# Three of four transposes of a squared-ReLU MLP's inner values in rounded fp32, from copies that a DMA makes

## The chip, the cores and the metric

The kernel runs on one core of one Trainium2 chip. The metric is the device time of one execution in microseconds; lower is better. Of each kernel several executions are timed, and one more is recorded by the hardware profiler; that one gives the profile and the trace.

The core has a matrix engine (TensorE, PE in the profile; its weight loads are PEld), three engines for vectors (VectorE: DVE, ScalarE: ACT, GpSimd: POOL) and SyncE (SP), which here only issues DMAs. All work from an on-chip memory of 128 partitions; TensorE writes to PSUM banks of 128 x 512 fp32.

## The reference

Two layers over 256 positions of width 2048: in the first the mixer is latent attention, in the second a state-space scan. After each mixer comes a dense MLP with a squared ReLU. Only the two MLPs matter here:

```python
def squared_relu_mlp(h, w_in, w_out):
    u = jax.nn.relu(h @ w_in)
    return (u * u) @ w_out

# in reference(), for each layer i:
    h = rms_norm(x, mlp_norm_g[i])
    x = x + squared_relu_mlp(h, mlp_w_in[i], mlp_w_out[i])   # w_in 2048 x 8192, w_out 8192 x 2048
```

All inputs are fp32.

## The kernel before

**Products in halves.** TensorE multiplies in rounded fp32 (`F32R`). To keep fp32's precision each operand is split into a rounded high half and the rest: ScalarE writes `wh` (L102), VectorE subtracts it and writes `wl` (L103). A product is three matmuls, high x high, high x low, low x high (L594, L595, L596 in the MLPs; L325, L326, L329 elsewhere). The weights come by DMA from SyncE's queue (L85), are split some units ahead, and are the moving operand; the activations are the stationary one, so they have to stand transposed, 128 inner values on the partitions.

**One MLP.** The 8192 inner values are worked on in 8 pairs of blocks of 512, for two halves `t` of the positions. Pair 0 is computed directly (token `c`). Pairs 1 to 7 take seven products of combined quarters in place of eight (tokens `s`, named M1, N7, N5, N6, N4, M2, N3), whose sums VectorE forms (`sub` and `plus`, L598 and L599). The quarters of the weights are combined by VectorE (L183) and, once for each of four steps, by a DMA of GpSimd that adds to a tile (L199). Between the tokens of pair p run those of the out-projection of the pair before (`o`, four column blocks, of which the last falls into the pair after).

**A turn.** When the sums of a block are there, ScalarE takes the ReLU (L602) and the square (L546, in `hidden`) in a 128 x 512 scratch tile `r`. A *turn* then brings the tile into the stationary form: `transposed` (L306 to L311) makes four transposes of 128 x 128 on TensorE (L310) into one PSUM bank of the pool `sm`, and `split_out` has ScalarE write the high half (L299) and VectorE the low half (L300). There are four turns in a pair, for e, w, m1 and c in the code's names: after N6, N4, M2 and N3. `transpose` is given the data and the fp32 identity `self.ident`.

**The order.** TensorE runs in the order in which the program is written; that of the other engines is made by the compiler's scheduler, from the order of the program. `plan()` writes out the order of the tokens. `mlp_body` goes through them with a clock of its own, `at[0]`, which `move` advances by TensorE's time of the products (1.36 us for an `s` token, 2.72 for the others). `turn` (L578) puts the transposes on a list with a due time: the clock plus 10, 8, 7, 7 or 5 us (`TR`), and at least 4 us (`TR_GAP`) after the turn before. `move` issues whatever is due after a token.

**Buffers.** The pool `sm` has two banks; the turns and N7's accumulation share them. A bank is free when both halves have been written from it. The pool `mp` belongs to one MLP; the scratch tiles `s2` are seven.

Of the kernel before, what the change touches and what calls it, by code (L numbers as in the profile page):

```python
# [20 lines left out]
F32 = mybir.dt.float32  # L21
F32R = mybir.dt.float32r
# [6 lines left out]
P = 128  # L29
# [185 lines left out]
class Trunk:  # L215
# [90 lines left out]

    def transposed(self, src, h, lo, wide=True):
        b = self.bank(wide)
        for j in range(4):
            self.nc.tensor.transpose(b[:, j * P:(j + 1) * P], src[:, j * P:(j + 1) * P], self.ident)  # L310
        self.split_out(h, lo, b.rearrange("p (k n) -> p k n", k=4))  # L311


# [225 lines left out]
    def mlp_body(self, mp, layer, gain):  # L539
        nc = self.nc  # L540
        xa, rs = self.xT, self.rs
        us = {}

        def hidden(r, pp, j, t):

            nc.scalar.activation(r, r, AF.Square)  # L546
            if (pp, j) not in us:
                us[pp, j] = (self.ktile(self.k4), self.ktile(self.k4))
            h, lo = us[pp, j]
            return lambda wide: self.transposes(r, h, lo, t, wide)  # L550

        def relu(src, t):
# [12 lines left out]
        out, bank, v, count = {}, {}, {}, {}  # L565
        due = []
        at = [0.0, 0.0]
# [10 lines left out]
        def turn(r, p, j, t, us):  # L578

            fn = hidden(r, p, j, t)  # L580
            at[1] = max(at[0] + us, at[1] + TR_GAP)
            due.append((at[1], lambda: fn(False)))

        def pair_of_banks(pool):
# [20 lines left out]
        def after(name, p):  # L605
            if name == "M1":
                v["m1"] = self.scratch()
                nc.scalar.activation(v["m1"], bank["M1"], AF.Copy)
            elif name in ("N5", "N6"):
                v[name] = p  # L610
                if v.get("N5") != p or v.get("N6") != p:
                    return
                w, c, e = (self.scratch() for _ in range(3))
                sub(w, bank["N6"], v["m1"])
                plus(c, bank["N5"], w)
                plus(w, bank["N7"], w)
                plus(e, bank["N7"], c)
                v["w"], v["c"] = w, c
                turn(relu_in_place(e, 1), p, 1, 1, TR[0])
            elif name == "N4":  # L620
                sub(v["w"], bank["N4"], v["w"])
                turn(relu_in_place(v["w"], 1), p, 0, 1, TR[1])
            elif name == "M2":
                plus(v["m1"], bank["M2"], v["m1"])
                turn(relu_in_place(v["m1"], 0), p, 0, 0, TR[2])
            elif name == "N3":
                plus(v["c"], bank["N3"], v["c"])
                turn(relu_in_place(v["c"], 0), p, 1, 0, TR[3])
# [5 lines left out]
        for tok in tokens:  # L634
            key = (tok[0], layer) + tok[1:]
            if tok[0] == "s":
                _, p, name, d = tok
# [12 lines left out]
            elif tok[0] == "c":  # L650
                _, p, j, o = tok
# [11 lines left out]
            else:  # L663
                _, p, nb, o = tok
# [701 lines left out]
LATE5 = ()  # L1366
TR = (10, 8, 7, 7, 5)
TR_GAP = 4
PAUSE = 2.7


def merged(p, blocks):
# [21 lines left out]
    while main or late or second or units:  # L1394
        op = next((q for q in (late, main, second) if q and ready(*q[0])), None)
        filler = t >= rest and len(units) > (4 if p == 7 and op else 0)
        if filler and (op is None or work > t * ve / pe - 2):
# [3 lines left out]
            if not units or units[0][0] != b:  # L1401
                rest, work = t + (PAUSE if b[0] == "o" else 10), work + 1.37
        else:
# [160 lines left out]
```

## Time and profile before

| | us |
|---|---|
| median of 3 runs | 2293.53 (2292.96 to 2295.82) |
| the profiled execution | 2294.05 |
| its span, first to last instruction | 2292.3 |
| DVE (VectorE) busy | 1907.0 |
| ACT (ScalarE) busy | 1392.6 |
| POOL (GpSimd) busy | 212.7 |

The page has busy times, the span in 40 slices, the DMA queues, the chain of work that ended last, the costliest groups of instructions and the DMA issues. A group's row gives the line, the engine, what is written and read, the shape and the count; then busy time and the mean duration of one in ns; then the idle time of the engine before them and what ended it. Matmuls are pipelined: a record's duration is longer than the distance to the next start. In a timeline the columns are start, duration, engine, line, operation and count.

### The profile page before, as it was taken

The numbers are of one execution on the slowest core, as the hardware profiler recorded it, in microseconds if no ns is written. First come the engines' busy times: TensorE is split into PE (matmuls) and PEld (weight loads), VectorE is DVE, ScalarE is ACT, GpSimd is POOL, SyncE is SP. The second block draws the span as 40 slices with busy tenths as digits, with TensorE's granted clock in tenths as the row PEclk, the third lists the DMA queues.
The fourth block names the chain that finished last, engine by engine and source line by source line (L and its number), as shares of the span: only waits on it lengthen the run. The fifth ranks groups of instructions, "written<-read, shape, count | busy, mean of one in ns | idle before, by whom it ended". The sixth has DMA issues, their size and how long they took to land.

```text
span 2292.3 us, 30455 instructions
## 1 busy us (share of the span) xinstructions
PE 2283.9 (100%) x10929; PEld 1898.4 (83%) x10929; DVE 1907.0 (83%) x2318; ACT 1392.6 (61%) x1947; POOL 212.7 (9%) x229
## 2 busy tenths in 40 slices
PE   9999999999999999999999999999999999999999
PEld 7898888888888888888888888888888888888887
DVE  7785698999899898687898688676989889989895
ACT  7775476566566666564666545544666666666663
POOL 1430000000000000000133112120000000000000
PEclk9999999999999999999999999999999999999999
DMA  8445687877887878667877777666687788888874
GB/s 315 151 126 155 198 230 249 261 242 252 262 242 247 262 215 275 201 209 241 283 262 264 253 265 256 228 197 200 208 258 233 244 267 244 249 267 239 249 226 163
DMA packets 161912, 538.07 MB, mean 235 GB/s; under 512 B 17680, under 2 KB 26832, under 8 KB 160736
## 3 DMA queue, kind: packets, MB, share of 16 engines
q1 hardware_dynamic: 151264, 502.44, 66.2%
q0 software_dynamic: 8096, 29.41, 7.9%
q10 hardware_dynamic: 2400, 4.27, 0.5%
q8 instruction: 86, 1.41, 0.3%
q14 instruction: 66, 0.54, 0.1%
HBM read 529.65 MB, written 6.41 MB: 234 GB/s over the span
## 4 chain that ended last, share of the span: by engine, by line
PE 97%; DMA 1%; DVE 1%; issue 0%; ACT 0%; SPq 0%; DVEq 0%
PE acc L325 13%; PE acc L326 13%; PE acc L329 13%; PE yp L595 9%; PE yp L596 9%; PE yp L594 9%; PE st L595 7%; PE st L596 7%; PE st L594 7%; PE sm L310 2%; DMA wraw<-mi 1%; DVE wl L103 1%; PE y L1280 1%; PE acc L594 1%; PE acc L596 1%; PE acc L595 1%
## 5 line engine op out<-in xcount | busy, mean ns | idle before, releaser
L102 ACT ACTIVATE wh<-wraw 128x1024 fp32r<-128x1024 f32 (+1 forms) x818 | 858.2, 1053 | 607.3 <-PE acc L326 284.3
L103 DVE TENSOR_TENSOR wl<-wraw,wh 128x1024 fp32r<-128x1024 f32 (+1 forms) x818 | 986.4, 1221 | 230.2 <-ACT wh L102 220.8
L595 PE MATMUL yp<-wl,k 128*128 128x512 f32 x896 | 348.9, 389 | 2.0 <-DVE wl L103 2.0
L594 PE MATMUL yp<-wh,k 128*128 128x512 f32 x896 | 349.8, 390 | 0.0
L596 PE MATMUL yp<-wh,k 128*128 128x512 f32 x896 | 348.8, 389 | 0.0
L325 PE MATMUL acc<-wh,xt 128*128 128x512 f32 x704 | 279.1, 397 | 0.9 <-ACT wh L102 0.9
L326 PE MATMUL acc<-wh,xt 128*128 128x512 f32 x704 | 274.5, 390 | 0.3 <-DVE xt L463 0.3
L102 ACT ACTIVATE wh<-wrx 128x1024 fp32r<-128x1024 f32 x168 | 177.9, 1059 | 136.0 <-PE yp L596 107.1
L103 DVE TENSOR_TENSOR wl<-wrx,wh 128x1024 fp32r<-128x1024 f32 x168 | 204.4, 1222 | 35.6 <-ACT wh L102 35.3
L595 PEld LDWEIGHTS yp<-wl,k 128*128 128x128 f32 x896 | 168.2, 188 | 37.4 <-DVE wl L103 2.8
L596 PEld LDWEIGHTS yp<-wh,k 128*128 128x128 f32 x896 | 168.2, 188 | 35.0
L594 PEld LDWEIGHTS yp<-wh,k 128*128 128x128 f32 x896 | 168.2, 188 | 34.7
L325 PE MATMUL acc<-wh,k 128*128 128x512 f32 x496 | 196.5, 396 | 0.0
L326 PE MATMUL acc<-wh,k 128*128 128x512 f32 x496 | 193.2, 390 | 0.0
L329 PE MATMUL acc<-wl,xt 128*128 128x512 f32 x704 | 188.3, 389 | 0.0
L594 PE MATMUL st<-wh,xt 128*128 128x512 f32 x448 | 176.8, 395 | 0.0
L595 PE MATMUL st<-wl,xt 128*128 128x512 f32 x448 | 174.8, 390 | 0.0
L596 PE MATMUL st<-wh,xt 128*128 128x512 f32 x448 | 174.8, 390 | 0.0
L325 PEld LDWEIGHTS acc<-wh,xt 128*128 128x128 f32 x704 | 132.3, 188 | 29.9 <-ACT wh L102 2.2
L326 PEld LDWEIGHTS acc<-wh,xt 128*128 128x128 f32 x704 | 132.3, 188 | 28.5 <-issue 1.2
L329 PEld LDWEIGHTS acc<-wl,xt 128*128 128x128 f32 x704 | 132.2, 188 | 27.7
L199 POOL DMA_DIRECT2D wrx<-mi x56 | 49.1, 876 | 1142.1 <-DVE wl L103 1036.1
(307 smaller groups left out, 3447.9 us busy)
## 6 DMA issues: line engine op xcount, KB each, us to landing
wraw<-mi SPq DMA_DIRECT2D x256, 512.0 KB, 5.3
wraw<-mo SPq DMA_DIRECT2D x256, 512.0 KB, 5.5
wraw<-si SPq DMA_DIRECT2D x160, 512.0 KB, 4.9
wraw<-so SPq DMA_DIRECT2D x64, 512.0 KB, 4.8
wrx<-mi SPq DMA_DIRECT2D x56, 512.0 KB, 5.3
wrx<-mi POOLq DMA_DIRECT2D x56, 512.0 KB, 8.2
wraw<-wo SPq DMA_DIRECT2D x32, 512.0 KB, 3.8
taps<-xD SPq DMA_DIRECT2D x16, 768.0 KB, 8.7
```

The source lines that it names most:

```text
L102: self.last = nc.scalar.activation(h[:, v], raw[:, v], AF.Copy)
L103: self.last_lo = nc.vector.tensor_tensor(lo[:, v], raw[:, v], h[:, v].bitcast(F32), ALU.subtract)
L199: nc.gpsimd.dma_start(st["b11"].tile, quarter(d, 1, 0), accum_op=ALU.add)
L310: self.nc.tensor.transpose(b[:, j * P:(j + 1) * P], src[:, j * P:(j + 1) * P], self.ident)
L325: nc.tensor.matmul(accs[t][:, :n], ah, wh[:, q, :], start=first and kt + q == 0, stop=False)
L326: nc.tensor.matmul(accs[t][:, :n], al, wh[:, q, :], start=False, stop=False)
L329: nc.tensor.matmul(accs[t][:, :n], lhs(kt + q, t)[0], wl[:, q, :], start=False, stop=en and q == nk - 1)
L594: nc.tensor.matmul(b, ah, wh, start=first and q == 0, stop=False)
L595: nc.tensor.matmul(b, ah, wl, start=False, stop=False)
L596: nc.tensor.matmul(b, al, wh, start=False, stop=last and q == 1)
L1280: nc.tensor.matmul(y[t][c, o], part(t)[:, c], xg[g][t][:, o], start=True, stop=True)
```

## The change

In pairs 1 to 6 of each MLP, once the square is there, GpSimd's DMA copies the first 384 of the 512 columns, word for word, into a tile of type `F32R` (four buffers). The turn's first three transposes read that tile, use an identity in `F32R` and write the bank as `F32R`; the fourth reads `r` in plain fp32 as before. The due time of these turns is 8 us later. The identity is copied once per MLP by GpSimd. Pairs 0 and 7 and all other transposes stay as they were.

```diff
     def transposed(self, src, h, lo, wide=True):
         b = self.bank(wide)
+        src, words = src if isinstance(src, tuple) else (src, None)
         for j in range(4):
-            self.nc.tensor.transpose(b[:, j * P:(j + 1) * P], src[:, j * P:(j + 1) * P], self.ident)
+            v = slice(j * P, (j + 1) * P)
+            if words is not None and j < 3:
+                self.nc.tensor.transpose(b.bitcast(F32R)[:, v], words[:, v], self.ident_r)
+            else:
+                self.nc.tensor.transpose(b[:, v], src[:, v], self.ident)
         self.split_out(h, lo, b.rearrange("p (k n) -> p k n", k=4))
...
         us = {}
+        self.ident_r = mp.tile([P, P], F32R, name="identr")
+        nc.gpsimd.tensor_copy(self.ident_r, self.ident)
...
             h, lo = us[pp, j]
+            if pp in WORDS:
+                q = mp.tile([P, 384], F32R, tag="tr", name=self.name("tr"), bufs=4)
+                nc.gpsimd.dma_start(q.bitcast(F32), r[:, :384])
+                r = (r, q)
             return lambda wide: self.transposes(r, h, lo, t, wide)
...
             fn = hidden(r, p, j, t)
-            at[1] = max(at[0] + us, at[1] + TR_GAP)
+            at[1] = max(at[0] + us + (COPY if p in WORDS else 0), at[1] + TR_GAP)
             due.append((at[1], lambda: fn(False)))
...
 TR_GAP = 4
+WORDS = range(1, 7)
+COPY = 8
 PAUSE = 2.7
```

## The prediction

> **What bounds the kernel now.** I read the page first (busy shares, granted clock, the chain that ended last), with the group of the transposes from the view by line and shape; then what the engines waited for; then the timeline of TensorE around one turn.
>
> ```profile
> PE 2283.9 (100%) x10929; PEld 1898.4 (83%) x10929; DVE 1907.0 (83%) x2318; ACT 1392.6 (61%) x1947; POOL 212.7 (9%) x229
> PEclk9999999999999999999999999999999999999999
> PE 97%; DMA 1%; DVE 1%; issue 0%; ACT 0%; SPq 0%; DVEq 0%
> ```
> ```profile
> L310 PE MATMUL sm<-cst,s 128*128 128x128 f32 x396 | 57.1, 272 | 0.0
> ```
>
> TensorE is busy for the whole span, at full clock, and the chain is 97% TensorE. So time goes only with TensorE's own instructions, and with waits that it does not have now. The transposes at L310 are a small group: 57.1 us for 396, and not all are touched.
>
> ```profile
> PE yp L595 <- DVE wl L103: 2.0, 2, 1.1
> DVE wraw L183 <- DMA wraw<-mi: 24.2, 24, 3.6
> ```
>
> In the MLPs TensorE waited only twice, 2.0 us in all, for a low half of a weight. VectorE waited 24 times for late weights, 24.2 us in all, and nearly all of it was absorbed before it reached TensorE.
>
> A matmul's record holds its pipeline latency, so what it costs is the distance between starts. This is one turn (four transposes between ordinary products):
>
> ```profile
> 644.26 0.39 PE L595 MATMUL yp<-wl,k 128*128 128x512 f32 x1
> 644.48 0.39 PE L596 MATMUL yp<-wh,k 128*128 128x512 f32 x1
> 644.71 0.60 PE L310 MATMUL sm<-cst,s 128*128 128x128 f32 x4
> 645.07 0.48 PE L594 MATMUL yp<-wh,k 128*128 128x512 f32 x1
> 645.38 0.39 PE L595 MATMUL yp<-wl,k 128*128 128x512 f32 x1
> 645.62 0.40 PE L596 MATMUL yp<-wh,k 128*128 128x512 f32 x1
> ```
>
> Ordinary starts lie 0.227 us apart. From 644.71 to 645.38 there are 0.67 us, of which one product takes 0.227: a turn costs about 0.45 us. The four records last 0.60 in sum and 272 ns each by the L310 row, so the starts lie (600 - 272) / 3 = 109 ns apart. A turn is four times 109 ns and some 15 ns at the change.
>
> **The change, part by part.** Pairs 1 to 6 of two layers, four turns in each: 48 turns, in each of which three of the four transposes change type. So 144 transposes count.
>
> *The shorter transposes.* No row shows a transpose of rounded fp32, so I go by how the moving columns are priced in the two types. L344 and L596 move rounded fp32; L932 and L1232 move plain fp32.
>
> ```profile
> L596 PE MATMUL yp<-wh,k 128*128 128x512 f32 x896 | 348.8, 389 | 0.0
> ...
> L1232 PE MATMUL sm<-s,cb 128*128 128x512 f32 x16 | 8.2, 590 | 0.0
> ...
> L344 PE MATMUL sm<-xt,wh 128*128 128x256 f32 x32 | 4.2, 283 | 0.0
> ...
> L932 PE MATMUL sm<-xt,xt 128*128 128x128 f32 x16 | 3.1, 273 | 0.0
> ```
>
> Plain: (590 - 273) / 384 = 0.83 ns a column. Rounded: (389 - 283) / 256 = 0.41 ns, half. The transpose of today (272) sits on the plain line (273 for the same 128 columns), and its distance, 109 ns, is 128 columns at 0.83 and next to nothing more. What does the rounded line give for the distance?
>
> ```profile
> 29.23 2.08 PE L344 MATMUL sm<-xt,wh 128*128 128x256 f32 x16
> ```
>
> (2080 - 283) / 15 = 120 ns for 256 columns and 227 ns for 512: 107 ns for 256 more, and 13 ns that do not depend on the columns. For 128 columns that is 53 + 13 = 66 ns. The other bound comes from the weight loads.
>
> ```profile
> L310 PEld LDWEIGHTS sm<-cst,s 128*128 128x128 f32 x396 | 48.3, 141 | 9.9
> ...
> L932 PEld LDWEIGHTS sm<-xt,xt 128*128 128x128 f32 x32 | 5.4, 191 | 0.4
> L344 PEld LDWEIGHTS sm<-xt,wh 128*128 128x128 f32 x32 | 4.1, 191 | 0.2
> ```
>
> A transpose's load is recorded with 141 ns, a rounded product's with 191. If a rounded transpose loads like a product, the load may set the pace, and all that the rows say is that it is no slower than L344's 120 ns. So the distance lies between 53 ns (columns alone) and 120 ns. I take 66: plain products have the 191 ns load too, so the shorter load goes with the transposing and not with the type. Saving: 3 x (109 - 66) = 0.13 us a turn, **6.2 us** over 48 turns. By the ends: 8.1 us saved, or 1.6 us lost.
>
> The Trainium skill speaks against this: "TensorE: Matmul & The Clock Gate", part 4 on the PE-mode transpose, puts a transpose at about 275 ns in a kernel and 173 of these down to access latency that dominates. The 272 ns agree, but by the 109 ns between starts the latency is overlapped; by the page alone the saving would be near nothing.
>
> *The word copy.* In each turn GpSimd issues a DMA of 128 x 384 words (192 KB) from the squared values, after ScalarE's square, and three transposes wait for its landing.
>
> ```profile
> wrx<-mi POOLq DMA_DIRECT2D x56, 512.0 KB, 8.2
> ...
> xD<-s POOLq DMA_DIRECT2D x1, 48.0 KB, 2.6
> ```
>
> GpSimd's transfers land in 2.6 us (48 KB) and 8.2 us (512 KB, adding to what is there). In proportion 192 KB give 2.6 + 5.6 x 144 / 464 = 4.3 us, an estimate; the ends are 2.6 and 8.2. The Trainium skill, "DMA: Bandwidth & Descriptors", anatomy of one DMA on the SWDGE path, would give 2.0 us and 0.45 us for the bytes; the 8.2 us, for which it would give 3.2, say that here it is too little.
>
> How much time is there? Pair 4, first layer: the squares on ScalarE and the turns on TensorE (the third, at 644.71, stands above).
>
> ```profile
> 624.54 0.63 ACT L546 ACTIVATE s<-s 128x512 f32<-128x512 f32 x1
> ...
> 634.55 0.63 ACT L546 ACTIVATE s<-s 128x512 f32<-128x512 f32 x1
> ...
> 640.16 0.62 ACT L546 ACTIVATE s<-s 128x512 f32<-128x512 f32 x1
> ...
> 646.97 0.62 ACT L546 ACTIVATE s<-s 128x512 f32<-128x512 f32 x1
> ```
> ```profile
> 627.45 0.60 PE L310 MATMUL sm<-cst,s 128*128 128x128 f32 x4
> 638.80 0.60 PE L310 MATMUL sm<-cst,s 128*128 128x128 f32 x4
> 649.27 0.60 PE L310 MATMUL sm<-cst,s 128*128 128x128 f32 x4
> ```
>
> Square's end to turn: 2.3, 3.6, 3.9 and 1.7 us. Following the planner's clock (1.36 us a token of a combined product, 2.72 of another; a turn goes out at the first token past its due time), COPY = 8 moves the first three turns of a pair by six tokens' worth, 8.16 us, and the fourth, which also has to keep TR_GAP, by 9.52. So the copy has 10.4, 11.8, 12.1 and 11.2 us. It needs 4.3, at most 8.2: **no wait**. The cover ends at a landing 10.4 us after the square.
>
> *GpSimd's queue.* Behind a waiting copy stand the adding DMAs of L199, on which the N4 products depend.
>
> ```profile
> 614.26 0.88 POOL L199 DMA_DIRECT2D wrx<-mi  x1 [18.24 <-DVE wl L103]
> 654.46 0.87 POOL L199 DMA_DIRECT2D wrx<-mi  x1 [39.32 <-DVE wl L103]
> ```
>
> Between 614.26 and 654.46 GpSimd did nothing, and all four squares of the pair end in that time (625.2 to 647.6). An issue takes 0.87 us. Cost: none.
>
> *The later turns.* Each turn takes one of two small banks and gives it back when VectorE has written the low half (L300).
>
> ```profile
> 647.15 0.69 DVE L300 TENSOR_TENSOR k<-sm,k 128x512 fp32r<-128x512 f32 x1
> ...
> 652.29 0.69 DVE L300 TENSOR_TENSOR k<-sm,k 128x512 fp32r<-128x512 f32 x1
> ```
>
> From a turn's start to that: 3.1 us (644.71 to 647.84) and 3.7 us (649.27 to 652.98). With the shift the third and fourth turns of a pair fall behind the start of the next pair's N7, which holds the other bank for long, so both use one bank, 5.44 us apart by the planner (4.08 in pair 6) and a turn's 0.33 us more: enough by 2 us, in pair 6 by 0.7. The out products that read the values now come 8.16 us after the third turn (6.8 in pair 6) and not 16.3: also enough. I cost both at nothing; were VectorE 3 us later, each of 12 pairs would lose up to 1 us.
>
> *The waits themselves.* Transposes now wait for a DMA too.
>
> ```profile
> L310 PEldq EVENT_SEMAPHORE  x76: 51/51/1211, 45.4 to 2240.5; - x76
> ```
>
> Such a wait takes 51 ns in the sequencer; the turn above lost nothing by it on the way in (644.48 to 644.71 is an ordinary step). Between 66 ns transposes it might show: 0 to 48 x 51 ns = 2.4 us. I take 0, as in the turns of today.
>
> *The transfers.* 48 x 192 KB run beside the weight loads.
>
> ```profile
> 641.00:651.00 10.00, 10.00 (x50) 8.29 (x49) 10.00 (x11) 6.47 (x9) 0.00 (x0) 1.00 0.65 206
> 651.00:661.00 10.00, 10.00 (x46) 8.28 (x45) 9.91 (x11) 6.39 (x7) 0.87 (x1) 1.00 0.74 197
> ```
>
> The DMA share is 0.65 and 0.74 where the last two copies of a pair run, so there is room; but the next pair's first weights are those for which VectorE waits already, and 192 KB at some 300 GB/s hold them up by 0.65 us. In 12 pairs that is 0 to 7.8 us; only the 2 waits that reach TensorE today have no cover, so I take two such places at 0.5 us: **+1.0 us**.
>
> *The rest:* the rounded identity is one small copy per MLP on an idle GpSimd, the first turn that needs it comes, by the planner, some 90 us later; nothing.
>
> **Sum.** The profiled execution took 2294.05 us (span 2292.3 and 1.75 around it). 2294.05 - 6.2 + 1.0 = 2288.85. It lies 0.5 us above the median of 2293.53, so on the median's scale about **2288.4 us**, 0.22% less. The bound that a measurement can tell is 0.2%, 4.6 us: the line lies at 2288.9, and my forecast hardly passes it.
>
> **The rivals.**
> - *The transposes get no shorter.* The load of 191 ns, or a transposing rate that does not depend on the type, keeps the distance at 109 to 120 ns. For it: the two load rows, and that no row shows such a transpose (also the skill's rule above). Against: half the price of a column in each rounded row. Time: 2293.5 + (0 to 1.6) + 1.0, so 2294 to 2296.
> - *The gain goes into new waits.* Turns 1 us late in one bank, or 0.65 us of late weights in more pairs, or 51 ns in each turn. For it: VectorE is full in 641 to 651 (10.00 of 10.00). Against: margins of 2 us. Time: 2288.4 + 2 to 5, so 2290.5 to 2293.5.
> - *The copies are late; slower.* TensorE stops in order at the transposes. The loss of a pair is what the landing exceeds 10.4, 11.8, 12.1 and 11.2 us by, summed. At 10.8 us it eats the gain (0.4 x 12 = 5 us); at 11.5 us it is 1.4 x 12 = 17 us: 2305; at 12.5 us 4.5 x 12 = 54 us. For it: GpSimd's transfers are the slowest of all in the list of DMAs beside their size. Against: 8.2 us for over twice the bytes.
>
> **How the numbers follow.** Forecast 0.54, of which 0.42 on the far side of 2288.9 and 0.12 on the near side, since the 53 ns end and an absent wait pull down (to 2285) and the 51 ns up. No shorter: 0.19, of which 0.03 over 2298.1 (with late weights in several pairs). New waits: 0.14, all within. Late copies: 0.13, slower. So faster 0.42, within 0.2% 0.42 (0.12 + 0.16 + 0.14), slower 0.16. The range runs from 2285.0 (8.1 us saved, nothing lost) to 2297.5, leaving out the late copies and little else. The forecast's own range is 2285.0 to 2290.5.
>
> **What would show it.** Right: the three transposes start 66 ns apart and a turn costs 0.32 us, not 0.45; copies land in 3 to 6 us, TensorE has no wait for them; the waits of L595 for L103 stay at 1 to 4 us. Wrong: a distance of 109 or more; waits of TensorE at the transposes named by the copy's DMA, or by L300; a longer list of waits for late weights.

## The result

| | before | changed |
|---|---|---|
| median of 10 runs, us | 2294.13 (2292.39 to 2296.86) | 2288.68 (2286.92 to 2289.81) |
| span of the profiled execution, us | 2292.3 | 2287.5 |

The ratio is 0.9974, 95% interval 0.9965 to 0.9984: 3.7 to 8.0 us less. (The ten runs of before, on the chips of this comparison, have a median 0.6 us above the three that the prediction started from.) The forecast was 2288.4.

The page of the changed kernel, busy shares and chain, then the transposes in the view by line and shape (L313 the rounded ones, L315 the plain ones):

```profile
PE 2280.0 (100%) x10929; PEld 1893.7 (83%) x10929; DVE 1906.0 (83%) x2318; ACT 1391.2 (61%) x1947; POOL 243.0 (11%) x279
...
PE 95%; DVE 2%; DMA 2%; ACT 1%; issue 1%; POOL 0%; SPq 0%; ACTq 0%; DVEq 0%
```
```profile
L315 PE MATMUL sm<-cst,s 128*128 128x128 f32 x252 | 42.7, 277 | 0.0
...
L313 PE MATMUL sm<-identr,tr 128*128 128x128 f32 x144 | 17.8, 233 | 0.0
```

TensorE is still busy throughout, so the time came off TensorE's own work: 144 transposes have moved to L313, and a record there lasts 233 ns on average and not 272. What counts is the distance between starts. One turn of the changed kernel, on TensorE and on its weight loads:

```profile
645.79 0.40 PE L607 MATMUL yp<-wh,k 128*128 128x512 f32 x1
646.02 0.37 PE L313 MATMUL sm<-identr,tr 128*128 128x128 f32 x3
646.23 0.30 PE L315 MATMUL sm<-cst,s 128*128 128x128 f32 x1
646.28 0.48 PE L605 MATMUL st<-wh,xt 128*128 128x512 f32 x1
646.60 0.39 PE L606 MATMUL st<-wl,xt 128*128 128x512 f32 x1
646.83 0.40 PE L607 MATMUL st<-wh,xt 128*128 128x512 f32 x1
```
```profile
645.79 0.46 PEld L313 LDWEIGHTS sm<-identr,tr 128*128 128x128 f32 x3
646.20 0.14 PEld L315 LDWEIGHTS sm<-cst,s 128*128 128x128 f32 x1
646.23 0.21 PEld L605 LDWEIGHTS st<-wh,xt 128*128 128x128 f32 x1
646.37 0.19 PEld L606 LDWEIGHTS st<-wl,xt 128*128 128x128 f32 x1
```

From the first transpose to the second product behind the turn there are 0.58 us (646.02 to 646.60); before the change 0.67. The three rounded transposes take 0.21 us up to the plain one; single starts in the trace are 60, 62 and 85 ns apart in nearly all 48 turns, and a whole turn costs 359 ns where it cost 452. So 93 ns x 48 = 4.5 us. The waits of TensorE and VectorE, and the copies (the last line gives the shortest, median and longest time from issue to landing):

```profile
PE st L606 <- DVE wl L103: 0.7, 2, 0.4
```
```profile
DVE wraw L183 <- DMA wraw<-mi: 17.9, 20, 2.4
```
```profile
DMA to landing us min/median/max: 2.1/5.1/7.2
```

TensorE waits for no copy, and for low halves of weights 0.7 us, not 2.0. The 4.5 us of the turns and some of those 1.3 us are the 4.8 us of the span.

### The profile page after: what moved, and what is told of

It reads as the page before. It is cut to its first block, busy times and chain, and to the rows that moved or that the text cites. A ratio compares the mean times of both kernels' runs of the same rounds, so it can differ in the third digit from the quotient of the medians.

```text
span 2287.5 us, 30624 instructions
## 1 busy us (share of the span) xinstructions
PE 2280.0 (100%) x10929; PEld 1893.7 (83%) x10929; DVE 1906.0 (83%) x2318; ACT 1391.2 (61%) x1947; POOL 243.0 (11%) x279
## 4 chain that ended last, share of the span: by engine, by line
PE 95%; DVE 2%; DMA 2%; ACT 1%; issue 1%; POOL 0%; SPq 0%; ACTq 0%; DVEq 0%
PE acc L330 13%; PE acc L331 13%; PE acc L334 13%; PE yp L606 9%; PE yp L607 9%; PE yp L605 9%; PE st L606 7%; PE st L607 7%; PE st L605 7%; DMA wraw<-mi 1%; PE sm L315 1%; DVE wl L103 1%; PE y L1291 1%; PE acc L607 1%; PE acc L605 1%
## 5 line engine op out<-in xcount | busy, mean ns | idle before, releaser
L334 PE MATMUL acc<-wl,k 128*128 128x512 f32 x496 | 132.7, 389 | 0.0
```

What stands on the lines that cost most here:

```text
L334: nc.tensor.matmul(accs[t][:, :n], lhs(kt + q, t)[0], wl[:, q, :], start=False, stop=en and q == nk - 1)
```

## The experiments

The theory at the start: the type of the transposes gives the gain, 93 ns a turn. That the weight loads set the pace was no part of it yet; it came with e4, whose expectation still takes 60 and 62 ns for every rounded transpose. The rival: the later turns give part of it, by another order of VectorE and the weights. Times are compared with runs of the kernel before on the same chips, whose median lay between 2293.5 and 2294.7 us. "Single" is one run.

| run | median, us | ratio to before, 95% interval |
|---|---|---|
| e1_plain_from_copy | 2295.01 | 1.0000, 0.9991 to 1.0009 |
| e2_delay_only | 2293.41 | 0.9997, 0.9988 to 1.0006 |
| e4_all_four | 2291.58 | 0.9986, 0.9977 to 0.9995 |
| e3_no_delay | 2390.92 | single |
| e5_plain_first | 2290.36 | 0.9985, 0.9976 to 0.9994 |
| e6_every_other | 2289.58 | 0.9982, 0.9973 to 0.9991 |
| e7_copy4 | 2297.16 | 1.0015, 1.0006 to 1.0023 |
| e8_twice | 2303.22 | single |
| e9_delay4_only | 2291.62 | 0.9984, 0.9974 to 0.9993 |
| e10_copy6 | 2289.75 | 0.9978, 0.9969 to 0.9987 |
| e11_copy4_plain | 2293.47 | 0.9994, 0.9985 to 1.0003 |
| e12_copy4_in_order | 2442.73 | 1.0655, 1.0640 to 1.0669 |

### One part at a time

Everything but the type (e1), and the delay alone (e2):

```diff
-                self.nc.tensor.transpose(b.bitcast(F32R)[:, v], words[:, v], self.ident_r)
+                self.nc.tensor.transpose(b[:, v], words.bitcast(F32)[:, v], self.ident)
```
```diff
             if pp in WORDS:
-                q = mp.tile([P, 384], F32R, tag="tr", name=self.name("tr"), bufs=4)
-                nc.gpsimd.dma_start(q.bitcast(F32), r[:, :384])
-                r = (r, q)
+                pass
```

> The whole change, delay and word copies too, but the three transposes read the copies in plain fp32. Theory (the type of the transposes gives the gain): a turn costs 0.45 us again, not 0.36, the 4.5 us of 48 turns are gone, and the time is 2293 to 2295, ratio to before 0.999 to 1.001. Rival (the later turns give a good part of it, since they leave VectorE and the weights a better order): 2289 to 2291, ratio 0.998.

> Only the 8 us of delay in pairs 1 to 6: no copies, all four transposes in plain fp32 from the squared tile. Theory (type): as before within 1 to 1.5 us, 2292.5 to 2294.5; the wait of TensorE for late weights may go from 2.0 to 0.7 us as in the changed kernel. Rival (later turns): 2289 to 2291. Against the run with plain transposes from the copies it gives the price of the copies: 0 to 1 us by the theory, 1 to 3 if 192 KB beside the weights cost something.

Ratios of 1.0000 and 0.9997: with the plain type the gain is gone, and a delay of 8 us alone gives nothing that can be measured. The rival falls for this delay; with 4 us it does not (e9, below). Between the two, in which VectorE and ScalarE have the same order, the copies' price is not told from zero (0.7 us by the ratios, within both intervals, 1.6 by the medians). e1 differs from the changed kernel in more than the type: the compiler has VectorE's instructions in another order at some places. e5, below, has no such difference.

### What sets the pace of a rounded transpose

All four rounded (e4), the plain one first (e5), every other one (e6), and the three rounded ones made twice (e8, whose first pass is overwritten):

```diff
-            if words is not None and j < 3:
+            if words is not None:                  # e4, copies of 512 columns
+            if words is not None and j > 0:        # e5, copies of the last 384
+            if words is not None and j % 2 == 0:   # e6
```
```diff
-        for j in range(4):
+        for j in range(4) if words is None else (0, 1, 2, 0, 1, 2, 3):   # e8
```

> All four transposes of a turn rounded, from copies of 512 columns (256 KB). Theory: the distances of 60 and 62 ns hold for all four and the change to plain fp32 within the turn (85 and 52 ns) is gone: a turn costs 0.25 to 0.28 us, a further 0.08 to 0.11 x 48 = 4 to 5 us, so 2283.5 to 2285, ratio 0.9955. Rival: the larger copies land later than 10.4 us after the square, or hold up the weights; then TensorE waits at the turns, and it is 2288 or more.

> Each of the three rounded transposes of a turn is made twice (0, 1, 2, 0, 1, 2, then the plain fourth); the first pass is only overwritten. Theory (load pace): from the third distance on all are 82 to 87 ns, so three more cost 0.25 us a turn, 48 turns 12 us: about 2300. Rival (60 to 62 ns is the pace and 85 the price of the change of type): six distances of 60 to 62, 0.18 us a turn, 9 us: 2297.

Four rounded ones, TensorE and weight loads, then the doubled three, both likewise:

```profile
647.56 0.46 PE L313 MATMUL sm<-identr,tr 128*128 128x128 f32 x4
647.85 0.46 PE L605 MATMUL st<-wh,xt 128*128 128x512 f32 x1
648.15 0.39 PE L606 MATMUL st<-wl,xt 128*128 128x512 f32 x1
```
```profile
647.33 0.54 PEld L313 LDWEIGHTS sm<-identr,tr 128*128 128x128 f32 x4
647.82 0.19 PEld L605 LDWEIGHTS st<-wh,xt 128*128 128x128 f32 x1
647.92 0.19 PEld L606 LDWEIGHTS st<-wl,xt 128*128 128x128 f32 x1
```
```profile
470.34 0.63 PE L313 MATMUL sm<-identr,tr 128*128 128x128 f32 x6
470.81 0.29 PE L315 MATMUL sm<-cst,s 128*128 128x128 f32 x1
```
```profile
470.11 0.71 PEld L313 LDWEIGHTS sm<-identr,tr 128*128 128x128 f32 x6
```

Six rounded ones take 0.47 us up to the plain one where three took 0.21: three more cost 0.26 us, 87 ns each and not 60. Their loads say why. The six end at 470.82, and one lasts 139 ns (median), so the last starts at 470.68. The first went out a whole product early (470.11); the second can start only when the first transpose does, at 470.34. From there to 470.68 are four distances: 85 ns each. The loads of a series follow each other 85 ns apart, and the transposes follow them. The 60 and 62 ns at the start of a turn come from the one load that was made ahead.

That it is not the other way round, loads that wait for transposes, the changed kernel shows. Its second and third load in the turn at 646.02, each in a narrow window:

```profile
646.03 0.14 PEld L313 LDWEIGHTS sm<-identr,tr 128*128 128x128 f32 x1
...
646.11 0.14 PEld L313 LDWEIGHTS sm<-identr,tr 128*128 128x128 f32 x1
```

In the plain turns of before each load starts 1 or 2 ns after the transpose ahead of it has started. In the rounded ones the third load starts 25 ns and the fourth 50 ns after it (medians of 48 turns): the transpose is under way, and what holds up the next load is the load before it.

The time of e8, 2303.22, is a single run; the distances carry the reading.

So e4's forecast was wrong: four rounded ones take 0.59 us to the second product (647.56 to 648.15), not less than the 0.58 with three. The load of the product behind the turn starts 0.10 us ahead of the next load (647.82, 647.92) and nothing hides it; behind a plain transpose, which holds the array for 109 ns, it is hidden. By its time e4 loses nearly half of the gain, some 2.8 us by the ratios. The turns explain 0.8 of these (16 ns each, medians over 48 turns). Its copies of 256 KB go with VectorE's waits for weights at 29.9 us and TensorE's for low halves at 1.7, and the order of VectorE differs too; which of these costs the rest is not shown.

The Trainium skill, "TensorE: Matmul & The Clock Gate", section on the back-to-back issue gap, says that in a stream of loads and matmuls both set the spacing, and gives about 81 ns for 128 columns; the 85 ns here agree.

> The plain transpose stands first in the turn and the three rounded ones after it (the copy is of the last 384 columns). Theory (weight loads set the pace of rounded transposes: 84 ns from load to load, and the load of the product behind the turn, 108 ns, lies open behind a rounded one but is hidden behind a plain one): starts 109, 60, 84 ns apart and the product behind it about 157 ns after the last, so a turn costs some 0.41 us against 0.36, and the time is 2290.5 to 2291.5. Rival (three rounded ones save 93 ns wherever they stand): 0.36 us a turn and 2288 to 2289.

> The first and the third transpose rounded, the second and the fourth plain; the copy stays at 384 columns. Theory (load pace): a load is hidden behind each plain transpose, so both rounded ones take 60 ns and none 85: 60 + 109 + 60 and the plain one's end, a turn costs 0.38 us, only 0.02 more than with three: 2289 to 2290. Rival (the saving goes with the number of rounded ones): two thirds of 93 ns, a turn costs 0.39 us and the time is 2290 to 2291. The distances in the trace tell them apart better than the time.

```profile
468.89 0.28 PE L315 MATMUL sm<-cst,s 128*128 128x128 f32 x1
468.93 0.46 PE L313 MATMUL sm<-identr,tr 128*128 128x128 f32 x3
469.22 0.46 PE L605 MATMUL st<-wh,xt 128*128 128x512 f32 x1
469.52 0.39 PE L606 MATMUL st<-wl,xt 128*128 128x512 f32 x1
```
```profile
468.34 0.22 PE L313 MATMUL sm<-identr,tr 128*128 128x128 f32 x1
468.41 0.28 PE L315 MATMUL sm<-cst,s 128*128 128x128 f32 x1
468.44 0.30 PE L313 MATMUL sm<-identr,tr 128*128 128x128 f32 x1
468.58 0.28 PE L315 MATMUL sm<-cst,s 128*128 128x128 f32 x1
468.61 0.48 PE L605 MATMUL st<-wh,xt 128*128 128x512 f32 x1
468.93 0.39 PE L606 MATMUL st<-wl,xt 128*128 128x512 f32 x1
```

With the plain one first (e5) it is 0.63 us to the second product, 0.05 more than with the plain one last: the same four instructions in another order give back half of the saving, as the load theory has it. (A record behind a plain one starts early and waits, as at 468.93.) With two rounded ones between plain ones (e6) it is 0.59, 0.01 more than with three: the saving does not go with their number. e6's time lies in its expected range, e5's 0.1 us below it.

e5 is the cleanest of these runs: VectorE and ScalarE have exactly the changed kernel's order in it, so only TensorE's own order within the turn (and which columns are copied) differs. Its 0.05 us a turn are 2.4 us over 48 turns; the ratios differ by 2.5 us, each known to some 2 us. The loads of e6 add a limit to the theory: behind the load of a plain transpose the next load follows after 62 ns (median of 48 turns), so the 85 ns belong to the loads of rounded transposes and not to every load.

### How much delay the copies need

```diff
-COPY = 8
+COPY = 0    # e3; 4 in e7, 6 in e10
```

> The change with COPY = 0: the turns stay where they were before. A copy lands 5.1 us after its issue (median of the changed kernel), and the turns of a pair come 2.3, 3.6, 3.9 and 1.7 us after the square: TensorE waits about 3.0, 1.7, 1.4 and 3.6 us, 9.7 a pair, 12 pairs, 116 us: about 2400. If the landing gets quicker while TensorE waits (weights come no faster than they are used), less: 2340 to 2400. If the delay is not needed: 2288 to 2292.

Without delay TensorE's waits and one such place, then the granted clock there (the column behind POOL's):

```profile
PE sm L313 <- DMA tr<-s: 75.0, 42, 3.3
```
```profile
464.42 0.39 PE L607 MATMUL yp<-wh,k 128*128 128x512 f32 x1
467.85 0.59 PE L313 MATMUL sm<-identr,tr 128*128 128x128 f32 x3 [3.04 <-DMA tr<-s]
...
469.33 0.63 PE L607 MATMUL st<-wh,xt 128*128 128x512 f32 x1
469.76 0.63 PE L605 MATMUL st<-wh,xt 128*128 128x512 f32 x1
```
```profile
468.00:471.00 3.00, 3.00 (x10) 2.46 (x11) 0.69 (x1) 0.60 (x1) 0.00 (x0) 0.50 0.65 210
471.00:480.00 9.00, 9.00 (x41) 7.42 (x40) 7.34 (x9) 7.06 (x8) 0.56 (x1) 0.99 0.50 153
```

The run took 96 us more than before; about 2400 in all was expected. The waits are 75.0 us of that. Beside them TensorE lost clock: here 3.43 us passed from the last product's start to the transposes, and then the products stood 0.43 us apart in place of 0.227, at a granted clock of 0.50, for some 3 us. The trace has twelve such stretches of 3.4 us between its first and last turn, so at half the clock some 20 us are lost, an estimate. Two other waits, and the granted clock behind each:

```profile
653.69 0.43 PE L313 MATMUL sm<-identr,tr 128*128 128x128 f32 x3 [3.23 <-DMA tr<-s]
...
863.37 0.43 PE L313 MATMUL sm<-identr,tr 128*128 128x128 f32 x3 [2.09 <-DMA tr<-s]
```
```profile
654.00:657.00 3.00, 3.00 (x16) 2.52 (x15) 0.93 (x2) 1.66 (x2) 0.00 (x0) 1.00 0.56 179
864.00:867.00 3.00, 3.00 (x8) 2.33 (x8) 0.69 (x1) 1.01 (x2) 0.00 (x0) 0.50 0.91 305
```

A wait of 3.23 us left the clock at 1.00 and one of 2.09 us halved it, so the length of a single wait does not decide; what does stays open. The Trainium skill, "TensorE: Matmul & The Clock Gate", section on HAM oscillation, puts the limit of an idle gap at some 3.4 us. This run does not bear out such a limit: the 3.43 us at the first place are near it, but the clock was halved after 2.09 us and not after 3.23 us.

> The change with a delay of 4 us in place of 8. In the changed kernel the copies landed 2.4 to 7.6 us after the square and at least 4.6 us ahead of their turn. Theory (the cover only has to reach the landing): nearly all copies still land in time, at most a few waits of under 1 us: 2288 to 2291. Rival (8 us are needed): waits of TensorE for the copies in most turns and 2295 or more.

> The change with a delay of 6 us. All copies should land in time (the latest landed 7.6 us after its square, the turns come at 8.3 and later). Theory A (place of the turns): the turns take other places than with 4 or 8, so anything between 2288 and 2297, with the waits for low halves making the difference to 2288 us plus or minus 1. Rival (a shorter delay costs in proportion): 2292 to 2293, half way.

With 4 us the copies are nearly all in time, and yet it is 2297: slower than before. The waits of TensorE with 4 us, then of VectorE, and those of TensorE with 6:

```profile
PE st L606 <- DVE wl L103: 4.1, 5, 1.1
...
PE sm L313 <- DMA tr<-s: 1.2, 4, 0.4
PE yp L606 <- DVE wl L103: 1.2, 2, 0.6
```
```profile
DVE wraw L183 <- DMA wraw<-mi: 35.7, 26, 2.5
```
```profile
PE sm L313 <- DVE k L300: 2.0, 3, 1.5
```

So the theory of e7 (only the landing counts) fell: 1.2 us of waits for copies, but 5.3 for low halves of weights, behind sums for which VectorE waits 35.7 us. Together these are 6.5 us of the 9.0 by which e7's span is longer than the changed kernel's (2296.5, 2287.5); the rest is not accounted for. With 6 us (2289.75) the low halves are in time, and 2.0 us go to a wait that the prediction had among its new ones: two turns close together (the second and third of a pair, some 3.1 us apart), the later one waiting for VectorE's L300.

> A delay of 4 us in pairs 1 to 6, no copies, all transposes plain. With 4 us the change took 2297.2 us, with 1.2 us of waits for copies and 5.3 for low halves of weights. Theory A (the place of the turns in the program puts VectorE and the weights out of order, with or without copies): 2298 to 2302 here, the 2297.2 and the 4.5 us of the types, with some 5 us of waits for low halves. Rival B (it takes the copies' transfers too): 2293 to 2295, as with the delay of 8 us alone.

> A delay of 4 us, with copies, the transposes plain from the copies. Theory A and B: 2298 to 2302, ratio 1.002 to 1.003, waits for low halves of some 5 us. If 2294 or less, the waits come with the rounded transposes alone, by neither of the two.

e9 and e11 are e2 and e1 with COPY = 4. Neither theory held: with copies and plain transposes it is 2293.47, no worse than before, and without copies 2291.62, quicker than before by some 3.7 us (ratio 0.9984, interval 0.9974 to 0.9993). So a delay of 4 us gives by itself over half of what the whole change gives with 8, with no transpose rounded. VectorE's order is another than before there, and its waits for late weights are 12.9 us, not 24.2:

```profile
DVE wraw L183 <- DMA wraw<-mi: 12.9, 12, 3.4
```

The copies cost 1.9 us between e9 and e11, by the medians; the two have the same order of VectorE and ScalarE. The 4 us are bad only together with the rounded type. e7 and e11 differ in it alone, but the compiler, which orders VectorE and ScalarE, put VectorE's instructions in another order at the change of pairs: in e7 sums that wait for a late weight (L183) stand ahead of low halves that are ready. To test that, e12 (e7 with one change) held each sum behind the low half that the program has before it:

```diff
-        add = lambda out, a, b: nc.vector.tensor_tensor(st[out].tile, st[a].tile, st[b].tile, ALU.add)
+        def add(out, a, b):
+            with flow.tc.issue_after(flow.last_lo.ins):
+                nc.vector.tensor_tensor(st[out].tile, st[a].tile, st[b].tile, ALU.add)
```

> The change with a delay of 4 us (2297.2 us), and VectorE's sums of weight quarters may not be issued ahead of the low half that the program has before them; so no sum that waits for a late weight stands ahead of low halves that are ready. Theory (the 8 us over the delay of 8 us come from VectorE's order at the change of pairs): the waits for low halves fall from 5.3 to 1 or 2 us and the time to 2288 to 2291. Rival (the weights themselves come later, whatever the order): the waits stay, 2295 or more. If the order held so costs at other places, it shows as waits of VectorE for weights or of ScalarE for the sums.

```profile
ACT wh L102 <- DVE wraw L186: 211.0, 90, 4.3
...
ACT wh L102 <- DVE wrx L186: 129.0, 47, 3.2
```

It took 2442.73: the sums now come so late that ScalarE waits 340 us for them, and TensorE's waits for low halves rise to 60.1 us at one line alone. It undoes more than the difference in question and tells nothing of it. That VectorE's order costs e7 its 8 us is what the traces suggest, and stays open.

## Why the prediction was right

The total was right to 0.3 us, and that is luck: two errors cancelled. 6.2 saved and 1.0 lost were forecast; 4.5 came from the turns, and the waits for weights gave a little more. (The lower end of the range, 2285.0, does not come out of its own sum: 2293.5 less 8.1 is 2285.4. Nothing hangs on it.)

- **Half price of a rounded column, so a shorter transpose:** right. The first distances are 60 and 62 ns, between the 53 ns of the columns and my 66.
- **The size of the saving:** wrong, and the term that was mis-sized. The step was the choice between the bounds: "plain products have the 191 ns load too, so the shorter load goes with the transposing and not with the type". That is so (L313's loads last 139 ns), but from it I took that the load does not bind at all. In a series loads follow 85 ns apart, more than the 66 that I took for the matmul; the third distance is 85, and the place of the plain one decides what the product behind pays. 93 ns a turn, not 129. L310's rows could not show it, since its 109 ns hide 85.
- **The copies in time:** right. Estimated 4.3 us; median 5.1, at most 7.2. The cover was 10.4 us and more (TensorE waits for no copy). Without it late copies stop TensorE as the third rival says, some 8 us a pair; 6.3 of these are the waits that the rival counts, and the lost clock, which it does not have, makes up most of the rest.
- **GpSimd's queue:** right; the 48 issues add little (POOL busy 243.0, not 212.7), and nothing waits for them.
- **The bank:** right for 8 us; with 6 us the second and third turn lie 3.1 us apart, nearer than the 4.08 that I called enough by 0.7, and 2.0 us show.
- **51 ns waits in the sequencer:** right at 0; the turn starts an ordinary step behind the last product (645.79 to 646.02).
- **Late weights, +1.0 us:** wrong in sign here (2.0 to 0.7 us), right as a danger: e7 pays 5.3 us. It goes with the order that the compiler makes, which no row of before tells; that the order is the cause is not shown.
- **The rivals:** "no shorter" fell to the distances, and to e1 against the changed kernel. The rule in part 4 of the Trainium skill's "TensorE: Matmul & The Clock Gate", by which access latency dominates a transpose's duration, did not tell its cost: the records are 272 and 233 ns long, the distances 109 and 60 to 85.

## What to carry over

For short matmuls the load of the stationary side has to be priced as well as the moving columns: of a row of quick ones only the first is free, and a slow one last in the row can hide the load of what follows, so the cheapest mix may keep one slow instruction, at the end. A wait that is moved out of the way by a delay has to be tried at several delays, since the delay also moves other engines' work and the compiler's order; here a delay alone moved the time by 0 to 3.7 us, nearly as much as the turns saved. Where the sum of small terms comes out right, look at the terms all the same.

## What was not expected

The distance of rounded transposes: 60 and 62 ns for the first, 82 to 88 in a series. The load of a product, left open behind a rounded transpose: 0.10 us to the next load (647.82 to 647.92). Waits of 2.09 and 3.04 us halved the granted clock for some 3 us, one of 3.23 us did not. A delay of 4 us with nothing else was quicker than before.
